# Scores of four query tiles in one run of six PSUM banks: a hybrid attention block on one Trainium2 core

## The chip, the cores and the metric

The kernel runs on one core of one Trainium2 chip. A core has five engines with queues of their own that work side by side: TensorE (PE) multiplies matrices, VectorE (DVE), ScalarE (ACT) and GpSimd (POOL) work element by element, SyncE (SP) issues the transfers (DMA). Matmul results land in PSUM, which the program uses as eight banks of 128 partitions by 512 single-precision columns; everything else lies in SBUF. The metric is the device time of one execution in microseconds (us); the median of three runs of the kernel before is 594.63 (594.57 to 594.85).

## The reference

One layer of a decoder block over 512 positions of width 1024, with 16 learned "meta" positions set in front (528 keys). Two attentions of 16 heads each run on the same normed input: MLA (queries and keys from low-rank latents, with a rotary part) and a "forgetting" attention (FoX below: a cumulative forget gate is added to the logits). Cut to what matters:

```python
u = rmsnorm(h, pre_norm_g[l])
proj = u @ w_in[l]                      # cq, ckv, k_pe, z_mla, fq, fk, fv, f_logit, z_fox, gates
q = (rmsnorm(cq) @ w_uq[l])...          # 16 heads: 64 + 32 rotary
kv = (rmsnorm(ckv) @ w_ukv[l])...       # 16 heads: 64 keys, 64 values
o_mla = causal_block_attention(q_m, k_m, v_mla, MLA_SCALE)
y_mla = (o_mla * silu(z_mla)) @ w_br_mla[l]
cum = cumsum(log_sigmoid(f_logit + fox_forget_b))
o_fox = causal_block_attention(fq, fk, fv, FOX_SCALE, cum)   # logit[t,s] += cum[t] - cum[s]
y_fox = (o_fox * silu(z_fox)) @ w_br_fox[l]
mixed = (sigmoid(gate_a) * y_mla + sigmoid(gate_b) * y_fox) @ w_out[l]
h = h + rmsnorm(mixed, post_norm_g[l])
```

The attention takes 128 queries at a time: query tile b (0 to 3) sees 144 + 128 b keys, 144, 272, 400 and 528.

## The kernel before

**Precision.** Every projection is done in three passes of fast-precision operands: weights and inputs are split into a high and a low part (`wh`, `wl`, `uTh`, `uTl`), and high x high, high x low, low x high are summed. ACT makes the high half of each 128 x 1024 block of weights (L130), POOL, or DVE where `low[0]` says so, the low half (L103). The same split makes `hlq`, `hlk` out of queries and keys.

**Stages.** The attention part runs over 16 stages, `stages = [(br, pr) for pr in range(NH // 2) for br in (1, 0)]`: pair of heads pr, FoX (br 1) and then MLA (br 0). Only PE's order is written out by hand; the other engines' queues are ordered by a scheduler from the order of the code, from priorities (`high_priority`) and from pins (`issue_after`), SP's transfers in program order. In a stage PE does:

- `scores(0)`: both heads side by side, one on each half of the array's rows (64 of 128), for query tiles 0, 1 and 2. Three pairs of matmuls for each piece in FoX, five in MLA (two for the rotary part, `QP`). Tiles 0 and 1 share a bank for each head (144 + 272 columns), tile 2 has one for each head (400 columns);
- `late`: the values' products `ov` of the stage before, 26 matmuls that use the array as two column halves, into the one bank of `ovp`;
- `scores(1)`: tile 3, 528 columns as 272 + 256 in two banks for each head;
- the fill: projections for the stage to come (q, k, v: `fq`, `fk`, `mq`, `mk`, `v`) and z, in steps of three matmuls. Their accumulators come from `accp`, three banks in rotation (`acc`).

PSUM so holds 3 banks `acc`, 4 banks `stp` in rotation for the scores and 1 bank `ovp`.

**Behind the scores.** DVE adds mask or forget bias, scales, and takes the row minimum in one pass out of PSUM (L784: `sf`, `nb`; the masks are `maskt`, or `cbp` and its masked copy `cbm`); ACT takes exponentials with their sums (L792); DVE the reciprocals (L800, L801). `norm(0)` (tiles 0 to 2) and `norm(1)` (tile 3) write the normed weights as a high and a low half-precision part: ACT L819 the high, DVE L820 the low, POOL the columns of the meta positions (the "lead", L806 to L811). Four DMA transposes for each stage (`pt<-pn`) bring them to the layout that the values' products need. `masked_bias` (POOL, L860 and L861) makes `cbm` for the next FoX stage behind the lead of `norm(1)`.

**Readers of the accumulators.** `hl_done` splits q and k out of the `acc` bank (ACT L244 high, DVE L103 low). v's two banks are read by DVE for the maximum (L688), by ACT (L701, L707) and by DVE (L710). z goes through ACT and DVE (L723, L724).

**Stage 0.** Before the loop stand the first k, q and v and a unit of gate projections (`gate_unit`, 8 steps of three matmuls, `pg`): four steps before the loop, three between `scores(0)` and `scores(1)`, one behind. Stage 0 has no values before it; their first products run in stage 1.

Of the kernel before, what the change touches and what calls it, by code (L numbers as in the profile page):

```python
# [25 lines left out]
L = S + META  # L26
# [19 lines left out]
HALF = 272  # L46
ROW = 64
# [7 lines left out]
def block_kernel(ctx: ExitStack, tc: tile.TileContext, x, meta_tokens, pre_norm_g, w_in, fox_forget_b,  # L55
# [119 lines left out]
    def unit(name, getw, act, nk, sls, done):  # L175
# [8 lines left out]
        for i, sl in enumerate(sls):  # L184
            n = sl.stop - sl.start
            for k in range(nk):
                def fn(i=i, sl=sl, k=k, n=n):
# [4 lines left out]
                    if k == 0:  # L192
                        st["ps"] = acc(f"{name}{i}")
# [11 lines left out]

    REAL = [slice(META, L)]
# [44 lines left out]
    def k_fox(pr):  # L251
        return unit(f"fk{pr}", win_w(O_FK, pr), u_act, KD, ALLT, hl_done(("k", 1, pr), L, HALF))

# [286 lines left out]
    with ExitStack() as att:  # L540
# [4 lines left out]
        stp = att.enter_context(tc.tile_pool(name="stp", bufs=4, space=PSUM))  # L545
        ovp = att.enter_context(tc.tile_pool(name="ovp", bufs=1, space=PSUM))

# [120 lines left out]
        def k_mla(pr):  # L668
            return unit(f"mk{pr}", lambda: by_k(mw[pr][2], 1), ckv_act, 1, ALLT, hl_done(("k", 0, pr), L, HALF))

        vsc = {}

        def v_unit(br, pr):
# [41 lines left out]
            return unit(f"v{br}{pr}", get, act, nk, ALLT, done), [(0, tr)]  # L715
# [15 lines left out]
        def attention(br, pr):  # L731
# [30 lines left out]
            def scores(g):  # L762

                banks = (((0, 0, 144, 0), (1, 0, 272, 144)), ((2, 0, 400, 0),)) if g == 0 else \
                    (((3, 0, HALF, 0),), ((3, HALF, L - HALF, 0),))

                def fn():
                    if g == 0:
                        for t in ("nb", "su", "ri"):
                            sums[t] = aw.tile([128, 2, 4], F32, tag=t, name=f"{t}{nm_}")  # L770
                    sfs[g] = aw.tile([128, 2, (2 * SF_STEP + 400, L)[g]], F32, tag=f"sf{g}", name=f"sf{nm_}{g}", bufs=1)
                    for ib, parts in enumerate(banks):
                        ps = [stp.tile([128, 512], F32, tag="st", name=f"st{nm_}{g}{ib}{h}") for h in range(2)]
                        for b, c0, w, o in parts:
                            for i, ops in enumerate(zip(*(sets(h, b, c0, w) for h in range(2)))):
                                for h, (Q, K) in enumerate(ops):
                                    mm(ps[h][:, o : o + w], Q, K, start=(i == 0), stop=(i == last_set))
                        for b, c0, w, o in parts:
                            for h in range(2):
                                nb = sums["nb"][:, h, b : b + 1]  # L780
                                for a, e, in1 in added(h, b, c0, c0 + w):

                                    with tc.high_priority(offset=100):
                                        nc.vector.tensor_tensor_reduce(  # L784
                                            out=sf_of(h, b)[:, a:e], in0=ps[h][:, o + a - c0 : o + e - c0],
                                            in1=in1, scale=-scale, scalar=3.0e38 if a == 0 else nb,
                                            op0=ALU.add, op1=ALU.min, accum_out=nb)
                    with tc.high_priority(offset=60):
                        for b in GRP[g]:
                            for h in range(2):  # L790
                                sf = sf_of(h, b)
                                exps[g] = nc.scalar.activation(sf, sf, AF.Exp, bias=sums["nb"][:, h, b : b + 1],  # L792
                                                               scale=-1.0, accum_out=sums["su"][:, h, b : b + 1]).ins
                return fn
# [521 lines left out]
```

## Time and profile before

| | |
|---|---|
| median of the runs | 594.63 us (594.57 to 594.85) |
| the profiled execution | 594.53 us, span 592.4 us |
| busy: PE / DVE / ACT / POOL | 583.9 / 412.8 / 357.9 / 200.6 us |
| scores on PE (`st`), share of the chain | 8% |
| values on PE (`ov`), share of the chain | 5% |
| `mk` on PE, share of the chain | 1% |

A row of the timeline is: start and length in us, engine, line, operation, written tile <- read tiles, shape, count. For PE "64*128" is a matmul on half the array's rows and "80*64" or "128*64" one on half its columns; the length of a matmul is modelled and overlaps the next, so the distance between two starts is the better measure. In square brackets stands how long the engine was idle before, and what ended it. A row of the chain is: start, length, engine, tile, line, number of instructions.

### The profile page before, as it was taken

What the parts mean: (1) busy time and instruction counts of PE and PEld (TensorE: products, weight loads), DVE (VectorE), ACT (ScalarE), POOL (GpSimd) and SP (SyncE); (2) the same over time, 40 slices, a digit from 0 to 9 for tenths busy, and PEclk for the clock granted to TensorE, in tenths of its full rate; (3) what the DMA queues carried; (4) which work ended last, traced back from release to release, by engine and by line L of the source; (5) the groups of instructions that cost most, each with busy time, mean ns of one, the idle gap of its engine ahead of it and who ended that gap; (6) DMA issues with size and microseconds to landing.
All of it is one profiled execution on the core that took longest, in us unless ns stands there. A gap on an engine that the chain in (4) does not pass through costs nothing.

```text
span 592.4 us, 11129 instructions
## 1 busy us (share of the span) xinstructions
PE 583.9 (99%) x3841; PEld 500.1 (84%) x3841; DVE 412.8 (70%) x1155; ACT 357.9 (60%) x816; POOL 200.6 (34%) x271
## 2 busy tenths in 40 slices
PE   8999999999999999999999999999999999999996
PEld 6889789889889888888898897888998998888884
DVE  5854876775775776666758748797647777468957
ACT  6946775784774784766748748764444363443753
POOL 4317746455458463554544544420000000000000
PEclk9999999999999999999999999999999999999999
DMA  8535599999994998997995986866822534333603
GB/s 282 125 88 164 120 176 251 225 184 237 168 205 111 229 205 197 213 182 179 185 202 147 203 160 147 193 138 215 273 72 71 143 97 134 91 106 106 214 2 142
DMA packets 220000, 97.47 MB, mean 165 GB/s; under 512 B 131456, under 2 KB 209672, under 8 KB 219944
## 3 DMA queue, kind: packets, MB, share of 16 engines
q1 hardware_dynamic: 219944, 96.77, 69.1%
q8 instruction: 30, 0.49, 0.3%
q14 instruction: 26, 0.21, 0.1%
HBM read 62.36 MB, written 3.97 MB: 112 GB/s over the span
## 4 chain that ended last, share of the span: by engine, by line
PE 97%; DMA 1%; DVE 1%; ACT 0%; SPq 0%; issue 0%; POOL 0%; DVEq 0%; POOLq 0%
PE z L97 19%; PE pg L97 15%; PE v L97 9%; PE st L97 8%; PE fk L97 8%; PE fq L97 8%; PE x L97 8%; PE py L97 7%; PE ov L97 5%; PE psm L97 3%; PE y L97 2%; PE mq L97 2%; PE mk L97 1%; PE ppe L97 1%; DMA wsr<-in_w_in_dram 1%; PE pt L100 0%
## 5 line engine op out<-in xcount | busy, mean ns | idle before, releaser
L103 POOL TENSOR_TENSOR wl<-wraw,wh 128x1024 fp32r<-128x1024 f32 (+2 forms) x62 | 120.3, 1948 | 96.3 <-ACT wh L130 74.0
L130 ACT CAST wh<-wraw 128x1024 fp32r<-128x1024 f32 (+1 forms) x72 | 74.6, 1040 | 53.5 <-PE py L97 16.8
L792 ACT ACTIVATE sf<-sf,nb 128x272 f32<-128x272 f32 (+3 forms) x128 | 72.5, 568 | 17.1 <-DVE nb L784 15.6
L820 DVE SCALAR_TENSOR_TENSOR pn<-sf,ri,pn 128x128 f16<-128x128 f32 (+3 forms) x128 | 68.6, 576 | 7.3 <-ACT pn L819 7.1
L103 DVE TENSOR_TENSOR wl<-wraw,wh 128x512 fp32r<-128x512 f32 (+1 forms) x54 | 51.0, 947 | 27.5 <-ACT wh L1053 18.9
L819 ACT ACTIVATE pn<-sf,ri 128x128 f16<-128x128 f32 (+3 forms) x128 | 61.2, 549 | 9.9 <-ACT sf L792 7.9
L97 PE MATMUL z<-uTh,wh 128*128 128x512 f32 x128 | 51.0, 398 | 0.0
L97 PE MATMUL pg<-uTh,wh 128*128 128x512 f32 x128 | 50.3, 393 | 0.0
L97 PE MATMUL z<-uTl,wh 128*128 128x512 f32 x128 | 50.1, 392 | 0.0
L97 PE MATMUL z<-uTh,wl 128*128 128x512 f32 x128 | 50.0, 391 | 0.0
L97 PE MATMUL pg<-uTl,wh 128*128 128x512 f32 x128 | 49.9, 390 | 0.0
L97 PE MATMUL pg<-uTh,wl 128*128 128x512 f32 x128 | 49.9, 389 | 0.0
L97 PE MATMUL st<-hlk,hlq 64*128 64x272 f32 (+3 forms) x480 | 45.5, 308 | 0.0
L1053 ACT CAST wh<-wraw 128x512 fp32r<-128x512 f32 x28 | 17.3, 619 | 39.8 <-DVE wraw L1062 15.4
L688 DVE TENSOR_REDUCE vsc<-v 128x1 f32<-128x272 f32 (+1 forms) x32 | 13.2, 433 | 39.9 <-PE v L97 39.9
L97 PEld LDWEIGHTS st<-hlk,hlq 64*128 64x128 f32 x480 | 34.5, 185 | 6.0 <-ACT vh L707 2.8
L97 PE MATMUL v<-uTh,wl 128*128 128x256 f32 (+1 forms) x128 | 36.5, 285 | 0.0
L97 PE MATMUL fk<-uTl,wh 128*128 128x256 f32 (+1 forms) x128 | 36.5, 285 | 0.0
L97 PE MATMUL fk<-uTh,wh 128*128 128x256 f32 (+1 forms) x128 | 36.4, 285 | 0.0
L97 PE MATMUL v<-uTl,wh 128*128 128x256 f32 (+1 forms) x128 | 36.4, 285 | 0.0
L97 PE MATMUL fk<-uTh,wl 128*128 128x256 f32 (+1 forms) x128 | 36.4, 285 | 0.0
L97 PE MATMUL v<-uTh,wh 128*128 128x256 f32 (+1 forms) x128 | 36.4, 284 | 0.0
(285 smaller groups left out, 1612.7 us busy)
## 6 DMA issues: line engine op xcount, KB each, us to landing
wraw<-in_w_in_dram SPq DMA_DIRECT2D x56, 512.0 KB, 4.7
cbp<-c_dram SPq DMA_DIRECT2D x16, 264.0 KB, 4.3
wraw<-in_w_br_fox_dram SPq DMA_DIRECT2D x8, 512.0 KB, 4.2
tb<-in_w_out_dram SPq DMA_DIRECT2D x8, 512.0 KB, 5.2
wraw<-in_w_br_mla_dram SPq DMA_DIRECT2D x8, 512.0 KB, 3.9
wraw<-in_w_out_dram SPq DMA_DIRECT2D x6, 512.0 KB, 3.8
xr<-in_x_dram SPq DMA_DIRECT2D x4, 512.0 KB
out_dram<-yo SPq DMA_DIRECT2D x8, 256.0 KB, 2.0
```

Of the source, the lines that this page charges most:

```text
L97: nc.tensor.matmul(*a, **k)
L103: return eng.tensor_tensor(out=lo, in0=src, in1=f32(hi), op=ALU.subtract)
L130: nc.scalar.copy(wh[:, :n], raw[:, :n])
L688: nc.vector.tensor_reduce(out=sc[:, i : i + 1], in_=ps, op=ALU.max, axis=AX.X, apply_absolute_value=True)
L792: exps[g] = nc.scalar.activation(sf, sf, AF.Exp, bias=sums["nb"][:, h, b : b + 1], scale=-1.0, accum_out=sums["su"][:, h, b : b + 1]).ins
L819: normed[:] = [nc.scalar.activation(hi, sf, AF.Copy, scale=rib).ins]
L820: nc.vector.scalar_tensor_tensor(out=lo, in0=sf, scalar=rib, in1=hi, op0=ALU.mult, op1=ALU.subtract)
L1053: nc.scalar.copy(to[0], src)
```

## The change

`stp` gets four banks with names of their own, b0, b1, c0, c1, instead of four in rotation. The scores of a stage become one run into six banks, three for each head: two `acc` banks hold tile 1 (272) and the first 240 columns of tile 3, b0 and b1 tile 0 (144) and tile 3's other 288, c0 and c1 tile 2 (400). The values' products of the stage before come behind that run and the fill behind them. Outside the scores the named banks serve as accumulators: FoX keys' first half in b0 (the second in `acc`), MLA keys' halves in b0 and b1, v's halves in c0 and c1. The exponentials are written in the order of tiles 1, 0, 2, 3. In stage 0 all eight gate steps stand ahead of the scores. The line numbers move by 1 to 10.

```diff
--- before.py
+++ after.py
@@ -44,6 +44,7 @@
 SF_STEP = 272
 PN_STEP = 5
 HALF = 272
+CUT = 240
 ROW = 64
 
 
@@ -172,7 +173,7 @@
 
     ths = {}
 
-    def unit(name, getw, act, nk, sls, done):
+    def unit(name, getw, act, nk, sls, done, banks=None):
 
         st = {}
         out = []
@@ -190,7 +191,7 @@
                         for load in getattr(out[0][1], "nxt", ()):
                             load()
                     if k == 0:
-                        st["ps"] = acc(f"{name}{i}")
+                        st["ps"] = (banks or acc)(f"{name}{i}")
                     ps = st["ps"][:, :n]
                     (wh, wl), (ah, al) = st["w"], act(k)
                     for q, (w, a) in enumerate(((wh, ah), (wh, al), (wl, ah))):
@@ -203,6 +204,7 @@
             out[0][1].load = getw.load
         return out
 
+    keybank = [None]
     REAL = [slice(META, L)]
     ALLT = [slice(0, HALF), slice(HALF, L)]
 
@@ -249,7 +251,7 @@
         return unit(f"fq{pr}", win_w(O_FQ, pr), u_act, KD, REAL, hl_done(("q", 1, pr), S, S))
 
     def k_fox(pr):
-        return unit(f"fk{pr}", win_w(O_FK, pr), u_act, KD, ALLT, hl_done(("k", 1, pr), L, HALF))
+        return unit(f"fk{pr}", win_w(O_FK, pr), u_act, KD, ALLT, hl_done(("k", 1, pr), L, HALF), keybank[0])
 
 
 
@@ -542,8 +544,16 @@
         att.enter_context(tc.manual_schedule(engines={mybir.EngineType.PE}))
         ac = att.enter_context(tc.tile_pool(name="ac", bufs=1))
         aw = att.enter_context(tc.tile_pool(name="aw", bufs=2))
-        stp = att.enter_context(tc.tile_pool(name="stp", bufs=4, space=PSUM))
+        stp = att.enter_context(tc.tile_pool(name="stp", bufs=1, space=PSUM))
         ovp = att.enter_context(tc.tile_pool(name="ovp", bufs=1, space=PSUM))
+
+        def bank(tag):
+            return lambda name: stp.tile([128, 512], F32, tag=tag, name=name)
+
+        def two(tag):
+            return lambda name: bank(tag + name[-1])(name)
+
+        keybank[0] = lambda name: bank("b0")(name) if name[-1] == "0" else acc(name)
 
         cb = [[thp.tile([128, L], F32, tag="th", name=f"cb{n}{h}") for h in range(2)] for n in "pm"]
         QP = ac.tile([128, S], F32R, tag="QP", name="QP")
@@ -666,7 +676,7 @@
         mw = {}
 
         def k_mla(pr):
-            return unit(f"mk{pr}", lambda: by_k(mw[pr][2], 1), ckv_act, 1, ALLT, hl_done(("k", 0, pr), L, HALF))
+            return unit(f"mk{pr}", lambda: by_k(mw[pr][2], 1), ckv_act, 1, ALLT, hl_done(("k", 0, pr), L, HALF), two("b"))
 
         vsc = {}
 
@@ -712,7 +722,7 @@
 
             def tr():
                 dma(vps[br], vh.rearrange("p t c -> p (t c)"), nc.sync.dma_start_transpose)
-            return unit(f"v{br}{pr}", get, act, nk, ALLT, done), [(0, tr)]
+            return unit(f"v{br}{pr}", get, act, nk, ALLT, done, two("c")), [(0, tr)]
 
         sils = {}
 
@@ -759,39 +769,36 @@
                 d = META + 128 * b if b else 0
                 return [(a, e, cb[n][h][:, a:e]) for n, a, e in ((0, c0, min(c1, d)), (1, max(c0, d), c1)) if a < e]
 
-            def scores(g):
-
-                banks = (((0, 0, 144, 0), (1, 0, 272, 144)), ((2, 0, 400, 0),)) if g == 0 else \
-                    (((3, 0, HALF, 0),), ((3, HALF, L - HALF, 0),))
-
-                def fn():
-                    if g == 0:
-                        for t in ("nb", "su", "ri"):
-                            sums[t] = aw.tile([128, 2, 4], F32, tag=t, name=f"{t}{nm_}")
+            def scores():
+
+                for t in ("nb", "su", "ri"):
+                    sums[t] = aw.tile([128, 2, 4], F32, tag=t, name=f"{t}{nm_}")
+                for g in range(2):
                     sfs[g] = aw.tile([128, 2, (2 * SF_STEP + 400, L)[g]], F32, tag=f"sf{g}", name=f"sf{nm_}{g}", bufs=1)
-                    for ib, parts in enumerate(banks):
-                        ps = [stp.tile([128, 512], F32, tag="st", name=f"st{nm_}{g}{ib}{h}") for h in range(2)]
-                        for b, c0, w, o in parts:
-                            for i, ops in enumerate(zip(*(sets(h, b, c0, w) for h in range(2)))):
-                                for h, (Q, K) in enumerate(ops):
-                                    mm(ps[h][:, o : o + w], Q, K, start=(i == 0), stop=(i == last_set))
-                        for b, c0, w, o in parts:
-                            for h in range(2):
-                                nb = sums["nb"][:, h, b : b + 1]
-                                for a, e, in1 in added(h, b, c0, c0 + w):
-
-                                    with tc.high_priority(offset=100):
-                                        nc.vector.tensor_tensor_reduce(
-                                            out=sf_of(h, b)[:, a:e], in0=ps[h][:, o + a - c0 : o + e - c0],
-                                            in1=in1, scale=-scale, scalar=3.0e38 if a == 0 else nb,
-                                            op0=ALU.add, op1=ALU.min, accum_out=nb)
-                    with tc.high_priority(offset=60):
-                        for b in GRP[g]:
-                            for h in range(2):
-                                sf = sf_of(h, b)
-                                exps[g] = nc.scalar.activation(sf, sf, AF.Exp, bias=sums["nb"][:, h, b : b + 1],
-                                                               scale=-1.0, accum_out=sums["su"][:, h, b : b + 1]).ins
-                return fn
+                for rooms, parts in (([acc, acc], ((1, 0, 272, 0), (3, 0, CUT, 272))),
+                                     ([bank("b0"), bank("b1")], ((0, 0, 144, 0), (3, CUT, L - CUT, 144))),
+                                     ([bank("c0"), bank("c1")], ((2, 0, 400, 0),))):
+                    ps = [room(f"st{nm_}{parts[0][0]}{h}") for h, room in enumerate(rooms)]
+                    for b, c0, w, o in parts:
+                        for i, ops in enumerate(zip(*(sets(h, b, c0, w) for h in range(2)))):
+                            for h, (Q, K) in enumerate(ops):
+                                mm(ps[h][:, o : o + w], Q, K, start=(i == 0), stop=(i == last_set))
+                    for b, c0, w, o in parts:
+                        for h in range(2):
+                            nb = sums["nb"][:, h, b : b + 1]
+                            for a, e, in1 in added(h, b, c0, c0 + w):
+
+                                with tc.high_priority(offset=100):
+                                    nc.vector.tensor_tensor_reduce(
+                                        out=sf_of(h, b)[:, a:e], in0=ps[h][:, o + a - c0 : o + e - c0],
+                                        in1=in1, scale=-scale, scalar=3.0e38 if a == 0 else nb,
+                                        op0=ALU.add, op1=ALU.min, accum_out=nb)
+                with tc.high_priority(offset=60):
+                    for b in (1, 0, 2, 3):
+                        for h in range(2):
+                            sf = sf_of(h, b)
+                            exps[b // 3] = nc.scalar.activation(sf, sf, AF.Exp, bias=sums["nb"][:, h, b : b + 1],
+                                                                scale=-1.0, accum_out=sums["su"][:, h, b : b + 1]).ins
 
             def norm(g):
                 def fn():
@@ -838,7 +845,7 @@
                 nc.vector.scalar_tensor_tensor(out=gT[br][:, pr, :], in0=po, scalar=vsc[br, pr], in1=sils[br, pr],
                                                op0=ALU.mult, op1=ALU.mult)
 
-            return scores(0), scores(1), norm(0), norm(1), values
+            return scores, norm(0), norm(1), values
 
         def stores(a, b):
 
@@ -887,8 +894,7 @@
         pe0, rest0, store0 = pe_unit(0)
         pe_rest = [(0, lambda x=x: rest0(x)) for x in range(2)]
         g = gate_unit()
-        first = pe0 + v + [(0, in_order)] + g[:4]
-        begun = g[4:]
+        first = pe0 + v + [(0, in_order)] + g
         fills = []
         for si, (br, pr) in enumerate(stages):
             last = si + 1 == len(stages)
@@ -897,7 +903,7 @@
             if br == 1:
 
                 za, zb = z_unit(1, pr), z_unit(0, pr)
-                fill = (vts[br, pr] if pr else begun) + za + q + zb[:3] + k + zb[3:5] + v + zb[5:]
+                fill = (vts[br, pr] if pr else []) + za + q + zb[:3] + k + zb[3:5] + v + zb[5:]
             elif not last:
 
                 fill = vts[br, pr] + q + k[:KD] + v + k[KD:]
@@ -921,34 +927,31 @@
         lctx.close()
         gpool = gctx.enter_context(tc.tile_pool(name="gpool", bufs=1, side="right"))
         gT += [gpool.tile([128, KD, S], F32, tag=n, name=n) for n in ("gT0", "gT1")]
-        run(first[len(pe0) : -4])
+        run(first[len(pe0) : -KD])
         behind[:] = [halved[("k", 1, 0), 1]]
-        run(first[-4:])
+        run(first[-KD:])
         behind.clear()
         late = []
         for si, (br, pr) in enumerate(stages):
             last = si + 1 == len(stages)
-            s0, s1, n0, n1, va = attention(br, pr)
+            sc, n0, n1, va = attention(br, pr)
 
             fill = fills[si]
-            for fn in [s0] + late:
+            sc()
+            for fn in late:
                 fn()
             if si == 0:
-                run(fill[:3])
-            s1()
-
-            if si == 0:
-
-                run(fill[3:5])
+
+                run(fill[:1])
                 run(vts[1, 0] + pe_rest)
                 n0()
                 bias(1)
                 low[0] = nc.vector
-                for ahead_ in [fn.prep for _, fn in fill[5:] if hasattr(fn, "prep")][:2]:
+                for ahead_ in [fn.prep for _, fn in fill[1:] if hasattr(fn, "prep")][:2]:
                     ahead_()
                 low[0] = nc.gpsimd
                 n1()
-                run(fill[5:])
+                run(fill[1:])
             else:
                 if si == 1:
                     stores(2, 4)
```

PE at the start of stage 1 (MLA). `st` are score banks, one number for each head, `ov` the values' bank; `z` is the projection ahead, `fq` the one behind. Before, from tile 2's last matmul through the values to tile 3 (the rows between repeat):

```order
L97 MATMUL st_1153<-KPL,QP 128x400
L97 MATMUL st_1154<-KPL,QP 128x400
...
L97 MATMUL ov_1173<-pt,vp_720 64x128
L97 MATMUL st_1202<-hlk_1074,hlq_1055 128x272
L97 MATMUL st_1203<-hlk_1074,hlq_1055 128x272
...
L97 MATMUL st_1202<-KPL,QP 128x272
L97 MATMUL st_1203<-KPL,QP 128x272
L97 MATMUL st_1216<-hlk_1074,hlq_1055 128x256
L97 MATMUL st_1217<-hlk_1074,hlq_1055 128x256
```

Now:

```order
L98 MATMUL z_1058<-uTh,wl_1005 128x512
L98 MATMUL st_1126<-hlk_1072,hlq_1053 128x272
L98 MATMUL st_1127<-hlk_1072,hlq_1053 128x272
...
L98 MATMUL st_1178<-KPL,QP 128x400
L98 MATMUL st_1179<-KPL,QP 128x400
L98 LDWEIGHTS vp_720
L98 MATMUL ov_1200<-pt,vp_720 64x512
...
L98 MATMUL ov_1200<-pt,vp_720 64x128
L98 MATMUL fq_1239<-uTh,wh_1233 128x512
```

The 272 and 256 columns of tile 3 stood between the values and the projection; now the values follow tile 2's 400 columns and the projection follows the values.

DVE in stage 0, behind the reads of v (`vh`) and ahead of the first reads of scores (ISA, `sf`). Before:

```order
L710 SCALAR_TENSOR_TENSOR vh<-v_814,vsc_812,vh 128x2x128
L784 ISA sf_873,nb_870<-st_874,cbm_707 128x144
L784 ISA nb_870 128x1
...
L784 ISA sf_921,nb_870<-st_933,cbm_708,nb_870 128x128
L784 ISA nb_870 128x1
L800 TENSOR_SCALAR su_871<-su_871 128x2x3
L801 RECIPROCAL ri_872<-su_871 128x2x3
L103 TENSOR_TENSOR wl_1007<-wraw_855,wh_1006 128x1024
```

Now:

```order
L720 SCALAR_TENSOR_TENSOR vh<-v_814,vsc_812,vh 128x2x128
L104 TENSOR_TENSOR wl_1005<-wraw_855,wh_1004 128x1024
L792 ISA sf_887,nb_884<-st_889,cbp_705 128x144
L792 ISA nb_884 128x1
L792 ISA sf_887,nb_884<-st_889,cbm_707,nb_884 128x128
L792 ISA nb_884 128x1
L792 ISA sf_888,nb_884<-st_889,cbp_705 128x240
```

The split of the weights `wl` that read `wraw_855` stood behind all reads of scores and the sums; now it is ahead of the first read.

POOL in stage 1: `mt` and `pn` are the lead columns (96 wide for tiles 0 to 2, 32 for tile 3), `wl` splits of the weights that `fk` (`wraw_1046`, now 1044) and `v` (`wraw_1058`, now 1056) of the same stage's fill use, `cbm` the masked bias. Before:

```order
L806 TENSOR_TENSOR mt_1258<-sf_1126,ri_1125 128x96
L809 CAST pn_715<-mt_1258 128x2x3x16
L811 CAST pn_715<-mt_1258 128x2x3x16
L810 TENSOR_TENSOR pn_715<-mt_1258,pn_715 128x2x3x16
L103 TENSOR_TENSOR wl_1294<-wraw_1046,wh_1293 128x1024
L103 TENSOR_TENSOR wl_1349<-wraw_1058,wh_1348 128x1024
L806 TENSOR_TENSOR mt_1312<-sf_1201,ri_1125 128x32
L809 CAST pn_716<-mt_1312 128x2x16
L811 CAST pn_716<-mt_1312 128x2x16
L810 TENSOR_TENSOR pn_716<-mt_1312,pn_716 128x2x16
L860 COPY cbm_707<-cbp_705 128x16
L861 AFFINE_SELECT cbm_707<-cbp_705 128x512
```

Now:

```order
L813 TENSOR_TENSOR mt_1308<-sf_1125,ri_1123 128x32
...
L817 TENSOR_TENSOR pn_716<-mt_1308,pn_716 128x2x16
L867 COPY cbm_707<-cbp_705 128x16
L868 AFFINE_SELECT cbm_707<-cbp_705 128x512
L867 COPY cbm_708<-cbp_706 128x16
L868 AFFINE_SELECT cbm_708<-cbp_706 128x512
L104 TENSOR_TENSOR wl_1290<-wraw_1044,wh_1289 128x1024
L813 TENSOR_TENSOR mt_1254<-sf_1124,ri_1123 128x96
...
L817 TENSOR_TENSOR pn_715<-mt_1254,pn_715 128x2x3x16
L104 TENSOR_TENSOR wl_1345<-wraw_1056,wh_1344 128x1024
```

Tile 3's lead and the masked bias went ahead of both splits, and the lead of tiles 0 to 2 between them.

## The prediction

> **What bounds the kernel now.** First the page's busy line and the chain that ended last.
>
> ```profile
> PE 583.9 (99%) x3841; PEld 500.1 (84%) x3841; DVE 412.8 (70%) x1155; ACT 357.9 (60%) x816; POOL 200.6 (34%) x271
> PE 97%; DMA 1%; DVE 1%; ACT 0%; SPq 0%; issue 0%; POOL 0%; DVEq 0%; POOLq 0%
> ```
>
> TensorE (PE) is the chain. A change can gain only by shortening PE's own sequence or by removing the few waits inside it, and it loses wherever PE comes to wait. So I read PE's starts one by one. This is the chain of waits at the start of a FoX stage (start, length, in us):
>
> ```profile
> 143.94 1.45 PE st L97 x18
> 145.38 1.97 PE ov L97 x26
> 147.35 1.11 PE st L97 x12
> ```
>
> Scores of tiles 0 to 2, the values' products of the stage before, scores of tile 3: 1.45 + 1.97 + 1.11 = 4.53. The timeline of PE shows the same start of an MLA stage operation by operation (start, length as modelled; the lengths overlap, so I use differences of starts):
>
> ```profile
> 120.29 0.39 PE L97 MATMUL z<-uTl,wh 128*128 128x512 f32 x1
> 120.52 0.39 PE L97 MATMUL z<-uTh,wl 128*128 128x512 f32 x1
> 120.84 0.56 PE L97 MATMUL st<-hlk,hlq 64*128 64x144 f32 x6
> 121.45 0.58 PE L97 MATMUL st<-hlk,hlq 64*128 64x272 f32 x6
> 122.12 0.71 PE L97 MATMUL st<-hlk,hlq 64*128 64x400 f32 x6
> 123.13 2.04 PE L97 MATMUL ov<-pt,vp 80*64 80x512 f16 x26
> 125.10 0.65 PE L97 MATMUL st<-hlk,hlq 64*128 64x272 f32 x6
> 126.18 0.28 PE L97 MATMUL st<-KPH,QP 64*128 64x256 f32 x2
> 126.30 0.28 PE L97 MATMUL st<-KPL,QP 64*128 64x256 f32 x2
> 126.51 0.50 PE L97 MATMUL fq<-uTh,wh 128*128 128x512 f32 x1
> 126.84 0.40 PE L97 MATMUL fq<-uTl,wh 128*128 128x512 f32 x1
> ```
>
> Projections run on the whole array and 0.23 us apart; scores use it as two row halves (64*128), values as two column halves (80*64). Each change of shape shows: 0.32 instead of 0.23 before the scores, 0.33 between the first two fq. From first st to first fq the stage takes 126.51 − 120.84 = 5.67.
>
> **The change part by part.**
>
> *One run of scores in an MLA stage, eight times.* The second run, 125.10 to 126.51, takes 1.41. Without a change of shape around it the same 272 columns took 0.67 (121.45 to 122.12) and the 256 columns cost 5 pairs at 0.12 (126.18 to 126.30) = 0.60, so 0.14 of it is entry and exit. The entry into the first run and its exit into the values stay, and so do the first slow fq intervals, provided that values followed by a projection cost what they do here, late in the program:
>
> ```profile
> 399.61 2.04 PE L97 MATMUL ov<-pt,vp 80*64 80x512 f16 x26
> 401.58 0.50 PE L97 MATMUL pg<-uTh,wh 128*128 128x512 f32 x1
> ```
>
> They do: 1.97 to the next start, as ahead of the scores (123.13 to 125.10). Tile 3 as 240 + 288 columns instead of 272 + 256 is the same sum, and a 272 instead of a 144 at the head I estimate at 0.01 dearer. I take 0.13 a stage: 8 x 0.13 = 1.0. Bounds: 0 (the exit comes back behind the values) and 0.2 each (entry and exit both go whole).
>
> *The same in a FoX stage, seven times* (stage 0 apart), with a wait on top. The same twelve matmuls that take 1.11 at 147.35 stand in stage 0, where no values come before them, at
>
> ```profile
> 63.30 0.99 PE L97 MATMUL st<-hlk,hlq 64*128 64x272 f32 x12
> 64.22 0.50 PE L97 MATMUL pg<-uTh,wh 128*128 128x512 f32 x1
> 147.44 0.34 DVE L784 CUSTOM_DVE_ANT_0 sf<-st,cbm,nb 128x128 f32<-128x128 f32 x1
> ```
>
> 0.92: the other 0.19 is a wait for a bank. Tile 3's second half takes the banks of tile 2, and VectorE (DVE) lets go of them only after the last read, 147.44 to 147.78. In six separate banks that wait has no object. 0.19 + 0.14 = 0.33 a stage: 7 x 0.33 = 2.3. Bounds 0.19 and 0.4 each.
>
> *Stage 0's two runs become one.* There both runs lie between projections, so one whole set of entry and exit goes: 0.09 ahead of the scores and 0.10 behind the first projection, as in the MLA rows, and within the run 0.92 less 3 x 0.12 + 3 x 0.13 = 0.75, that is 0.17. I take 0.34, with bounds 0.17 and 0.36.
>
> *Keys' accumulators leave the common banks.* The chain has eight pieces of six mk matmuls; the first two and the last:
>
> ```profile
> 74.11 0.74 PE mk L97 x6
> 115.74 0.98 PE mk L97 x6
> 369.59 0.94 PE mk L97 x6
> ```
>
> In stage 0 they take 0.74; the other seven 0.98, 0.98, 0.89, 0.94, 0.92, 0.96, 0.94: 1.43 of waiting, for the bank that mq's low half is still read from. Now each half has a score bank, drained long before. −1.4, bounds −1.4 and 0 (if hlq's readers hold something else).
>
> Sum of PE's gains: 1.0 + 2.3 + 0.34 + 1.4 = 5.1; by the bounds 1.5 to 6.2.
>
> *What may come late: accumulators of v in tile 2's banks.* DVE's last reads of v in an MLA stage:
>
> ```profile
> 120.85 1.02 DVE L710 SCALAR_TENSOR_TENSOR vh<-v,vsc,vh 128x16 f16<-128x16 f32 x3 [0.72 <-ACT vh L707]
> ```
>
> v is read by 121.87. Tile 2 will start some 2.6 behind 120.84 (0.67 + 0.6 + 0.6 + 0.7), at 123.4: slack 1.6, so the cost is nothing, and if v is read later, what exceeds 1.6. In a FoX stage tile 2 comes 2.0 after the start and v has been read sooner before it, slack about 1.5.
>
> *What will come late: stage 0.* All four late gate steps now stand ahead of the scores: 4 x 3 x 0.23 = 2.8, so the scores start at 62.3 instead of 59.56. And the split of the next weights (wl, 1.23) now stands in DVE's queue ahead of the scores' reads.
>
> ```profile
> 65.03 1.05 ACT L130 CAST wh<-wraw 128x1024 fp32r<-128x1024 f32 x1 [0.44 <-issue]
> 65.80 0.69 DVE L800 TENSOR_SCALAR su<-su 128x6 f32<-128x6 f32 x1
> 66.62 1.23 DVE L103 TENSOR_TENSOR wl<-wraw,wh 128x1024 fp32r<-128x1024 f32 x1
> 56.61 0.38 SPq L91 DMA_DIRECT2D wraw<-in_w_in_dram  x1
> wraw<-in_w_in_dram SPq DMA_DIRECT2D x56, 512.0 KB, 4.7
> 69.24 9.27 SPq L91 DMA_TRANSPOSE pt<-pn  x4
> 81.26 2.04 PE L97 MATMUL ov<-pt,vp 80*64 80x512 f16 x26
> 144.99 0.31 DVE L784 CUSTOM_DVE_ANT_0 sf<-st,cbm 128x144 f32<-128x144 f32 x1 [0.18 <-PE st L97]
> 149.90 0.35 DVE L784 CUSTOM_DVE_ANT_0 sf<-st,cbm,nb 128x128 f32<-128x128 f32 x1
> ```
>
> Those weights are asked for at 56.61 and land, by the median 4.7, near 61.3 to 62.3; ScalarE's (ACT) half 1.05, then DVE's 1.23: 64.5. DVE's reads of one FoX stage take 150.25 − 144.99 = 5.3 with a gap for the values between, some 4.5 without it: 69.0 (68.0 if the split is early, 69.8 with the 5.3). Before, they had ended when the sums began, 65.80, and the first transpose came 3.44 later, at 69.24. The same distance gives 72.4, and tile 2's exponentials, now the last, may add some tenths: I take 72.7, a shift of 3.5. The four hold SP's queue 9.27, before until 78.51, and the values stood at 81.26: the margin is 2.75 less the unshown landing of the last one, so between 0 and 2.75. Values now come behind all scores, 3.6 instead of 2.3 behind the stage's start, which itself is 0.34 sooner: 82.2, 1.0 later than before. Stall: 3.5 − 1.0 − (0 to 2.75) = 0 to 2.5; I take the middle, 1.1.
>
> *Behind it, in stage 1*, SP's next two weight loads are issued 3.5 later too, and POOL does tile 3's lead and the two masked biases ahead of the first weight split, and tiles 0 to 2's lead ahead of the second.
>
> ```profile
> 84.69 0.35 POOL L806 TENSOR_TENSOR mt<-sf,ri 128x96 f32<-128x96 f32 x1 [1.51 <-DVE ri L801]
> 85.93 5.01 POOL L103 TENSOR_TENSOR wl<-wraw,wh 128x1024 fp32r<-128x1024 f32 x2
> 93.53 0.69 POOL L860 COPY cbm<-cbp 128x16 f32<-128x16 f32 x1
> 95.42 0.64 POOL L861 TENSOR_SCALAR_AFFINE_SELECT cbm<-cbp 128x512 f32<-128x512 f32 x1
> 93.44 0.29 PE L97 MATMUL v<-uTh,wl 128*128 128x272 f32 x1
> ```
>
> Masks 93.53 to 96.06 = 2.5, tiles 0 to 2's lead 84.69 to 85.93 = 1.2, tile 3's by estimate two thirds of it, 0.8, splits 5.0: 9.5. This chain can begin when tile 3's sums are there; before, tile 0 to 2's were at 84.69, and I estimate 0.8 later for tile 3 in the longer run, 85.5, so the second split ends near 95.0 instead of 90.94. v's third matmul wants it at 93.44, moved by the gain of 0.5 and the stall of 1.1 to 94.1. Stall 0 to 1.8 (POOL's lengths are rough); I take 0.5.
>
> Sum: 594.53 (the profiled execution) − 5.1 + 1.6 = 591.0; it lies 0.1 under the median of the runs shown, 594.63, which I leave out.
>
> [...] The row-half rows show 0.09 to 0.15 at a change of shape. [...]
>
> **The rivals.**
>
> *The full gain, nothing late*: the margin behind the transposes is near 2.75 and POOL's splits come in time. 594.53 − 5.1 + 0.2 = 589.6. For it: the margin is not bounded from below by a row. Against it: a shift of 3.5.
>
> *The start ripples*: stall 2.5 at the values, 1.8 at v: 594.53 − 5.1 + 4.3 = 593.7. For it: both come from one late queue, and each was bounded by rows. Against it: the second shrinks as the first grows.
>
> *DVE's emptying sets every stage (slower)*. PE writes six banks in 2.6 (FoX) to 3.5 us (MLA), DVE reads a FoX stage's in 4.5, and tile 2, last read, must pass exponentials, reciprocals and norms before the first transposes. If these start later in every stage than the next values can bear, PE waits 15 times. The row is
>
> ```profile
> 152.85 8.46 SPq L91 DMA_TRANSPOSE pt<-pn  x4
> ```
>
> It decides once the transposes' queue, free at 161.31 there, stays busy up to the values; 0.23 us at each of 15 boundaries cancels what is left of the gain (3.5), and 0.6 at each is +9: 600. Against it: in that stage DVE's reads all end ahead of the norms already (150.25, first transpose 152.85), so tile 2 being last moves little, and values themselves come 1.0 to 1.3 later. [...]
>
> *Values into projections cost more than in the one place seen*: the exit returns 15 times at 0.14 to 0.2, −5.1 + 1.6 + 2.5 = 593.5.
>
> **How the numbers follow.** Forecast 0.55 (own range 590.0 to 592.2, mostly the two stalls), full gain 0.15, ripple 0.14, exits 0.07, slower 0.09. A measurement here tells 0.2%, 1.2 us, from no change: faster means under 593.4. Faster: 0.55 + 0.15 + half of the ripple and of the exits = 0.81; same: the other halves less a little, 0.09; slower 0.10. The range leaves out the slowest case and the far ends: 588.9 to 593.3.
>
> **What would show it.** In the profile of the changed kernel: 5.5 us (MLA) and 4.2 (FoX) from the first st to the first projection; six mk in 0.74 everywhere; no bank wait in st; PE idle ahead of ov near 82.2 by about 1, and ahead of v's third matmul near 94 by about 0.5; first transposes near 72.7. It is wrong if st waits for DVE in every stage, if the first projection after ov starts later than 1.97 behind it, or if the late transposes are still late in stage 2.

## The result, and the profile after

The changed kernel took 590.18 us (median of six, 589.89 to 592.53), the kernel before beside it 594.43 us (593.52 to 594.85): a ratio of 0.9939, 95% interval 0.9927 to 0.9952. Forecast were 591.0 us, with 588.9 to 593.3 as the range. In a later run beside other versions the same kernel took 591.32 us (590.74 to 592.51), ratio 0.9949 (0.9937 to 0.9961); its spread is taken up with the experiments on the clock.

The page's busy line and the chain that ended last, of the changed kernel:

```profile
span 587.9 us, 11120 instructions
PE 577.0 (98%) x3841; PEld 497.4 (85%) x3841; DVE 416.7 (71%) x1155; ACT 357.2 (61%) x816; POOL 200.4 (34%) x271
PE 90%; POOL 3%; DMA 2%; DVE 2%; ACT 1%; issue 1%; SPq 0%; DVEq 0%; POOLq 0%
```

TensorE is busy for 6.9 us less, but the span is shorter by only 4.5, and the chain now leaves PE in places. The chain of waits at an MLA stage, a FoX stage and at mk (start, length, in us) shows what was gained:

```profile
121.39 3.52 PE st L98 x50
124.91 1.97 PE ov L98 x26
126.88 0.43 PE fq L98
144.22 2.19 PE st L98 x30
146.41 1.97 PE ov L98 x26
148.37 1.81 PE z L98 x7
157.51 0.74 PE mk L98 x6
```

From the first score to the first projection an MLA stage takes 126.88 − 121.39 = 5.49 us instead of 5.67, a FoX stage 148.37 − 144.22 = 4.15 instead of 4.53, and mk 0.74 instead of 0.98. In stage 0, one run between two projections:

```profile
61.37 0.39 PE L98 MATMUL pg<-uTh,wl 128*128 128x512 f32 x1
61.69 2.26 PE L98 MATMUL st<-hlk,hlq 64*128 64x272 f32 x30
63.88 0.50 PE L98 MATMUL z<-uTh,wh 128*128 128x512 f32 x1
```

2.19 us, where the two runs took 1.46 and 0.92; the second entry and exit beside the projections, 0.2, went too.

And this is where some of it went back: the timelines of SyncE, VectorE and TensorE at the start, and the chain there.

```profile
72.59 8.35 SPq L92 DMA_TRANSPOSE pt<-pn  x4
62.69 1.36 DVE L104 TENSOR_TENSOR wl<-wraw,wh 128x1024 fp32r<-128x1024 f32 x1 [3.32 <-ACT wh L131]
77.59 6.00 DMA pt<-pn
83.73 2.04 PE L98 MATMUL ov<-pt,vp 80*64 80x512 f16 x26 [2.21 <-DMA pt<-pn]
```

The first transpose starts at 72.59 instead of 69.24, the last lands at 77.59 + 6.00 = 83.59, and TensorE stands idle for 2.21 us (2.3 between starts) before the first values.

The sum: 8 x 0.18 + 7 x 0.38 + 0.39 + 1.43 = 5.9 gained, 2.3 lost to the wait and 0.08 ahead of v: 3.5 net. The ratio makes 3.6 of 594.4; the medians lie 4.2 apart, the two profiled executions 4.5. Of these 4.5 us some 0.6 lies ahead of all changed work: the last gate matmul starts at 61.37, where 59.24 plus the four steps moved ahead (2.76) would make 62.0. The 0.4 that is left is spread over the stages, a few hundredths in each, and is not assigned to a cause.

### The profile page after: what moved, and what is told of

The parts are those of the page before. It is cut to its first block, busy times and chain, and to the rows that moved or that the text cites. A ratio compares the mean times of both kernels' runs of the same rounds, so it can differ in the third digit from the quotient of the medians.

```text
span 587.9 us, 11120 instructions
## 1 busy us (share of the span) xinstructions
PE 577.0 (98%) x3841; PEld 497.4 (85%) x3841; DVE 416.7 (71%) x1155; ACT 357.2 (61%) x816; POOL 200.4 (34%) x271
## 4 chain that ended last, share of the span: by engine, by line
PE 90%; POOL 3%; DMA 2%; DVE 2%; ACT 1%; issue 1%; SPq 0%; DVEq 0%; POOLq 0%
PE z L98 17%; PE pg L98 14%; PE v L98 8%; PE x L98 8%; PE fq L98 8%; PE fk L98 8%; PE py L98 7%; PE st L98 7%; PE ov L98 5%; PE psm L98 3%; PE y L98 2%; PE mq L98 2%; POOL wl L104 1%; DMA pt<-pn 1%; PE mk L98 1%
## 5 line engine op out<-in xcount | busy, mean ns | idle before, releaser
L800 ACT ACTIVATE sf<-sf,nb 128x272 f32<-128x272 f32 (+3 forms) x128 | 72.7, 569 | 10.9 <-DVE nb L792 10.1
L827 DVE SCALAR_TENSOR_TENSOR pn<-sf,ri,pn 128x512 f16<-128x512 f32 (+3 forms) x128 | 71.5, 625 | 2.4 <-ACT pn L826 2.4
L826 ACT ACTIVATE pn<-sf,ri 128x512 f16<-128x512 f32 (+3 forms) x128 | 59.6, 548 | 0.0
L98 PE MATMUL st<-hlk,hlq 64*128 64x272 f32 (+4 forms) x480 | 41.3, 299 | 0.0
L98 PEld LDWEIGHTS st<-hlk,hlq 64*128 64x128 f32 x480 | 33.0, 186 | 4.1 <-ACT vh L717 2.1
```

The costliest lines, as they stand in the source:

```text
L98: nc.tensor.matmul(*a, **k)
L800: exps[b // 3] = nc.scalar.activation(sf, sf, AF.Exp, bias=sums["nb"][:, h, b : b + 1], scale=-1.0, accum_out=sums["su"][:, h, b : b + 1]).ins
L826: normed[:] = [nc.scalar.activation(hi, sf, AF.Copy, scale=rib).ins]
L827: nc.vector.scalar_tensor_tensor(out=lo, in0=sf, scalar=rib, in1=hi, op0=ALU.mult, op1=ALU.subtract)
```

## The experiments

All of them start from the changed kernel.

**Gate steps back where they were.**

```diff
-        first = pe0 + v + [(0, in_order)] + g
+        first = pe0 + v + [(0, in_order)] + g[:4]
+        begun = g[4:]          # run behind the scores of stage 0
```

> The changed kernel, with stage 0's gate steps as before: four ahead of the scores, four behind them. My theory: the 2.2 us that TensorE waits ahead of the first values' products (81.5 to 83.7 in the changed kernel) comes from the scores of stage 0 starting 2.8 us later and from the split of weights ahead of their reads; with both gone the first transposes start near 69 instead of 72.6, TensorE does not wait there, and the time falls by 2.0 us (0.3 may come back at z, whose weights are now split later): 588.2. Rival: the transposes are late for another reason (their own landing, traffic): the wait stays above 1 us and the time within 0.7 us of the changed kernel's 590.2.

Measured 589.55 us (589.40 to 591.78), ratio 0.9927 (0.9914 to 0.9941). The wait ahead of the first values is gone, as expected, but only 0.6 us came back where 2.0 were expected; the time alone would have fitted the rival. The queue and what TensorE waited for instead:

```profile
68.79 9.60 SPq L92 DMA_TRANSPOSE pt<-pn  x4
71.85 0.50 PE L98 MATMUL z<-uTh,wl 128*128 128x512 f32 x1 [0.19 <-DVE wl L104]
94.00 0.39 PE L98 MATMUL v<-uTh,wl 128*128 128x272 f32 x1 [1.02 <-POOL wl L104]
```

0.3 to 0.4 between starts went to z, as foreseen, and 1.2 to v's third matmul, which was not. GpSimd's timeline shows why:

```profile
85.84 0.64 POOL L868 TENSOR_SCALAR_AFFINE_SELECT cbm<-cbp 128x512 f32<-128x512 f32 x1
87.17 2.39 POOL L104 TENSOR_TENSOR wl<-wraw,wh 128x1024 fp32r<-128x1024 f32 x1
89.53 0.79 POOL L813 TENSOR_TENSOR mt<-sf,ri 128x96 f32<-128x96 f32 x1
91.39 2.56 POOL L104 TENSOR_TENSOR wl<-wraw,wh 128x1024 fp32r<-128x1024 f32 x1
```

Masks, first split, lead, second split: the order that the prediction named, ending at 93.95. In the changed kernel the second split ends at about the same time, and v's third matmul costs only 0.08 more than its neighbours (0.21 instead of 0.13 to the next start). From the timelines of GpSimd and TensorE in the changed kernel:

```profile
91.81 2.58 POOL L104 TENSOR_TENSOR wl<-wraw,wh 128x1024 fp32r<-128x1024 f32 x1
94.46 0.38 PE L98 MATMUL v<-uTh,wl 128*128 128x272 f32 x1
```

There TensorE comes late anyway, because it has waited for the values. One late chain covered the other.

**The early split of weights off VectorE.** The line `low[0] = nc.vector` ahead of the early splits is left out, so GpSimd does that one.

> The changed kernel, with the one early split of weights on GpSimd instead of VectorE, so that VectorE reads stage 0's scores from about 62.9 on instead of 64.0; all eight gate steps stay ahead. My theory: the transposes start 1.1 us sooner and the wait ahead of the first values shrinks from 2.2 to 1.1: 589.1. Rival (only the gates count, the reads have slack): no change, 590.2. Rival (GpSimd's lead columns come late behind the split): slower by up to 1 us.

Measured 590.23 us (590.17 to 590.86), ratio 0.9933 (0.9921 to 0.9945).

```profile
63.05 0.31 DVE L792 CUSTOM_DVE_ANT_0 sf<-st,cbp 128x144 f32<-128x144 f32 x1 [3.32 <-PE st L98]
72.14 8.54 SPq L92 DMA_TRANSPOSE pt<-pn  x4
83.46 2.04 PE L98 MATMUL ov<-pt,vp 80*64 80x512 f16 x26 [1.60 <-DMA pt<-pn]
71.58 0.54 POOL L817 TENSOR_TENSOR pn<-mt,pn 128x96 f16<-128x96 f32 x1
```

and in the changed kernel:

```profile
72.16 0.40 POOL L817 TENSOR_TENSOR pn<-mt,pn 128x96 f16<-128x96 f32 x1
```

VectorE starts 1.0 after the scores instead of 2.3, but the transposes come only 0.8 sooner and the wait shrinks by 0.6, to 1.60. Exponentials and norms do follow VectorE: ScalarE begins the norms at 69.31 instead of 70.23, 1.3 sooner counted from the scores. The first transpose, though, starts 0.02 to 0.03 behind the end of GpSimd's lead of tiles 0 to 2 in both kernels (72.12 and 72.56). That lead starts only 0.9 sooner, since tile 3's lead stands ahead of it until 70.2, and takes 1.9 instead of 1.7. So GpSimd's lead is what comes late, as in the third rival, but not because of the split, which had ended at 68.6, and without making the kernel slower. The forecast of 1.1 was too much. The time itself is that of the first rival (590.2): 0.6 is not told from the changed kernel there, since the beginnings of executions differ by about as much (0.6 between the profiled ones of the kernel before and the changed kernel), and it is the trace that speaks against this rival.

**Two runs again, in the six banks.** Values go between tile 3's second part and tile 2.

```diff
+                    if parts[0][0] == 2:
+                        for fn in mid:          # the values of the stage before
+                            fn()
                     ps = [room(f"st{nm_}{parts[0][0]}{h}") for h, room in enumerate(rooms)]
```

> The changed kernel with its six banks, but with the values' products put between tile 3's second part and tile 2: two runs of scores again in every stage. My theory: each of 15 stages pays one entry and one exit, 0.19 us as the traces of before and after differ without the bank wait, 2.8 us; and the first values are wanted 1.1 us sooner while the transposes land as late, so 1.1 more: 594.1. In FoX stages the score matmuls show no bank wait. Rival (what was gained in a stage is the bank wait and the order, not the changes of shape): at most 1.1 us slower, 591.3.

Measured 599.71 us (597.83 to 601.64), ratio 1.0094 (1.0077 to 1.0111): slower than the kernel before. The stages without a wait show what was asked for, an MLA and a FoX stage from the timeline of TensorE:

```profile
127.24 0.65 PE L98 MATMUL st<-hlk,hlq 64*128 64x272 f32 x6
132.92 0.50 PE L98 MATMUL fq<-uTh,wh 128*128 128x512 f32 x1
150.26 1.71 PE L98 MATMUL st<-hlk,hlq 64*128 64x272 f32 x24
154.60 0.50 PE L98 MATMUL z<-uTh,wh 128*128 128x512 f32 x1
```

MLA 5.68: as much as the kernel before (5.67), 0.19 more than the changed kernel. FoX 4.34: 0.19 more than the changed kernel, 0.19 less than the kernel before. So an entry and an exit cost 0.19 in either kind of stage, the bank wait in FoX stages cost 0.19, and the six banks and other widths by themselves change nothing in an MLA stage. This part of the theory holds to the hundredth. The time does not: it is 5.6 us above the 594.1 expected. Where it went:

```profile
85.28 3.45 PE L98 MATMUL ov<-pt,vp 80*64 80x512 f16 x26 [3.22 <-DMA pt<-pn]
85.20:88.50 3.30, 3.22 (x25) 2.01 (x26) 0.00 (x0) 1.06 (x4) 0.00 (x0) 0.55 0.90 271
171.88 0.62 PE L98 MATMUL ov<-pt,vp 80*64 80x512 f16 x4 [0.53 <-DMA pt<-pn]
```

The first values wait 3.22, and behind that wait the same 26 matmuls take 3.4 instead of 2.0 us: in the second row, which is a stretch of the table by windows (length, busy time of PE, PEld, DVE, ACT, POOL, then the granted clock of TensorE, DMA share and GB/s), the clock is 0.55. And three later MLA stages wait ahead of their values as well (0.53 for a transpose here, then 0.62 and 0.81, for which the trace names nothing), and in stage 1 fk waits 1.36 for a split of GpSimd. Late transposes are what the prediction's third rival feared, but in a kernel that wants its values 1.0 us sooner than the changed one and has tile 2's scores behind them; which of the two makes them late is not separated.

**MLA keys' accumulators back in the common banks.** `two("b")` is left out of `k_mla`.

> The changed kernel with MLA keys' accumulators back in the three common banks. By the trace of the changed kernel the low half of mq is read until 76.16 in stage 0 and 118.61 in stage 2, 2.9 and 1.9 us behind the start of mk's second half, and 0.05 behind it in six later stages. My theory: stage 0 waits 2.9, which takes the place of the 2.2 us wait ahead of the first values, stage 2 waits 2.0, six stages 0.1 each: +3.3 us, 593.5. Rival (the wait is what it was in the kernel before): +1.4 us, 591.6. Rival (the bank is not what mk waited for): no change.

Measured 597.1 us (596.41 to 597.43), ratio 1.0045 (1.0033 to 1.0057): 7 us above the changed kernel, twice what was expected.

```profile
76.23 0.40 PE L98 MATMUL mk<-cTh,wh 128*128 128x272 f32 x1 [2.47 <-DVE sil L734]
78.06 0.63 PE L98 MATMUL z<-uTl,wh 128*128 128x512 f32 x1
76.20:80.00 3.80, 3.77 (x12) 3.22 (x13) 1.44 (x3) 0.76 (x2) 0.00 (x0) 0.55 1.12 209
98.38 0.39 PE L98 MATMUL v<-uTh,wl 128*128 128x272 f32 x1 [1.00 <-POOL wl L104]
121.65 0.39 PE L98 MATMUL mk<-cTh,wh 128*128 128x272 f32 x1 [1.25 <-DVE sil L734]
163.19 0.93 PE mk L98 x6
162.76 0.68 DVE L104 TENSOR_TENSOR hlq<-mq,hlq 128x512 fp32r<-128x512 f32 x1
163.50 0.38 PE L98 MATMUL mk<-cTh,wh 128*128 128x256 f32 x1
```

It is a bank that mk waits for, in every stage. In stages 0 and 2 it is that of z, read by VectorE behind the norms (2.47 and 1.25), where the expectation had mq's. In the six later stages it is mq's, as expected, with 0.2 each instead of 0.1: in the last two rows the second half of mk starts at 163.50, behind VectorE's read of mq, which ends at 163.44. The wait of stage 0 takes the place of the one ahead of the first values, as expected. What the expectation lacked: z's matmuls right behind it take 0.43 each (78.06 to the next at 78.49) instead of 0.23, at a clock of 0.55 over 3.8 us, and v's wait of 1.0 at 98.38 shows as soon as nothing hides it.

**The transposes made later by one more.** In stage 0 tile 0's transpose is issued twice.

> The changed kernel, with stage 0's first transpose (tile 0) issued twice: the three others start 1.35 us later, nothing else moves. My theory: the wait ahead of the first values is the landing of the last transpose, so it grows from 2.2 to 3.6 us; and since TensorE showed a granted clock near half for some 3.5 us behind waits of 2.6 and 3.3 us in two other runs, but not behind 2.2, such a stretch follows here and costs another 1.7: 593.2. Rival (the wait is priced at its own length): 591.5. Rival (the transposes are not what the values wait for): 590.2.

Measured 594.59 us (593.87 to 595.32), ratio 1.0006 (0.9997 to 1.0015).

```profile
72.85 11.39 SPq L92 DMA_TRANSPOSE pt<-pn  x5
80.85 5.11 DMA pt<-pn
86.10 3.63 PE L98 MATMUL ov<-pt,vp 80*64 80x512 f16 x26 [4.41 <-DMA pt<-pn]
85.00:89.00 4.00, 2.90 (x18) 1.74 (x20) 0.54 (x3) 1.85 (x6) 2.26 (x8) 0.62 0.92 248
```

The wait grew by 2.2, to 4.41, more than the 1.35 of the extra transpose: from the first issue to the last of the five lie 8.00 (72.85 to 80.85), 3.0 more than between those of the four in the changed kernel (72.59 to 77.59; why is not shown), and the last one landed 5.11 after its issue instead of 6.00. Behind it the values take 3.6 instead of 2.0, at a clock of 0.62 over 4 us. Together 3.8, and 4.4 in the time. Both parts of the theory hold, the size of the first was too small. The executions differ in their mean clock too: 0.994 to 0.996 at 593.9 to 594.3, 0.991 to 0.992 at 594.6 to 595.3. The profiled one is of the first kind, so what the others have beside its one slow stretch is not known.

**The changed kernel again**, beside the next one.

> The changed kernel itself, on the same chip and in turn with the next two, so that the three can be compared. Its wait ahead of the first values lay at 2.2 us in its profile, close under the 2.5 behind which the clock fell elsewhere; my theory: most executions near 590.0, some of them about 1.7 us longer with a lower mean clock (0.995 instead of 0.998). Rival: no such second group.

Measured 591.32 us (590.74 to 592.51). Its profiled execution took 591.32 with a mean clock of 0.994. The same place in this execution, and the stretch behind the wait in the first one:

```profile
83.56 3.13 PE L98 MATMUL ov<-pt,vp 80*64 80x512 f16 x26 [2.06 <-DMA pt<-pn]
87.22 0.63 PE L98 MATMUL fq<-uTl,wh 128*128 128x512 f32 x1
84.00:88.00 4.00, 4.00 (x28) 3.10 (x25) 2.17 (x8) 3.94 (x11) 2.61 (x9) 0.57 0.79 238
```

```profile
84.00:88.00 4.00, 4.00 (x36) 3.24 (x33) 2.07 (x8) 4.00 (x11) 2.63 (x9) 1.00 1.18 228
```

The wait is even shorter, 2.06 against 2.21, but here the clock falls to 0.57 in the mean of these 4 us, where it was 1.00, and 28 matmuls run instead of 36: about 1.4 us more by the time that stage 2 begins (v in stage 1 starts at 95.67 instead of 94.21). So a wait of 2.1 to 2.2 us cost its length in one execution of this kernel and 1.4 us on top in another. The two groups that the theory expected show only in part. Over both sets of executions, the three at a mean clock of 0.994 or 0.995 took 591.3, 591.7 and 592.5, as slow as expected or slower; but the eight at 0.997 to 0.999 took anything from 589.9 to 592.5, half of them over 590.7, and in this set none came near 590.0. So the clock is not the whole of the spread, and the rest is open.

**Four gate steps ahead, again**, in turn with the changed kernel.

> The kernel with four gate steps ahead and four behind, again. From the traces it is 0.7 us shorter than the changed kernel between the first scores and stage 3; with no long wait left its executions should not show the lower clock: 589.4. Rival: no difference to the changed kernel within 0.2 us.

Measured 589.76 us (589.37 to 590.21), ratio 0.9921 (0.9909 to 0.9933), clocks 0.998 and 0.999: the interval lies below that of the changed kernel in the same turn, 0.9937 to 0.9961. This version beats both kernels. Of the 1.6 us between the two medians the traces explain 0.7 without the clock; that the long wait, behind which the clock fell to 0.57 in one of two profiled executions, makes up the rest is likely but not shown, since the changed kernel's executions without the lower clock lie above this version too.

**Stage 1 put in order by hand**, in the version with four gate steps ahead: ScalarE's halves of k's and v's weights ahead of the norms, on GpSimd the lead ahead of the second split (`issue_after(lead)`), the masked bias behind both splits.

> The kernel of the run with four gate steps ahead, with stage 1 put in order by hand: ScalarE's high halves of k's and v's weights ahead of the norms, GpSimd's lead columns of tiles 0 to 2 ahead of the second split, the masked bias behind both splits. My theory: the 1.2 us by which that kernel waits at v's third matmul (92.8 to 94.0) is GpSimd's queue, in which the masked biases (1.5 us) stand ahead of the splits and the second split waits for ScalarE; with that gone v does not wait and up to 0.6 may come back ahead of stage 2's values, whose transposes then land close to when they are wanted: 0.6 to 1.2 us faster than that kernel, 588.4 to 589.0. Rival: the wait moves whole to stage 2's values: no change, 589.5.

> The kernel with stage 1 put in order by hand, again. From the traces 1.3 us shorter than the changed kernel between the first scores and stage 3: 588.8, and no execution with the lower clock. Rival: the same time as the kernel with four gate steps behind the scores.

Measured 589.23 us (588.92 to 589.72, four executions), ratio 0.9917 (0.9903 to 0.993); the second time 590.17 us (588.85 to 593.29, six), 0.9937 (0.9918 to 0.9955). In the first one's profile v no longer waits, and what is left in stages 0 and 1 is

```profile
71.63 0.50 PE L98 MATMUL z<-uTh,wl 128*128 128x512 f32 x1 [0.17 <-DVE wl L104]
82.22 2.04 PE L98 MATMUL ov<-pt,vp 80*64 80x512 f16 x26 [0.31 <-DMA pt<-pn]
```

The trace has what was expected, 1.3 us less than the changed kernel from the first scores up to stage 3, and 0.6 less than with the gate steps alone. The times do not: the second one is 1.4 above the expected 588.8, and one execution did show a lower mean clock, 0.995 at 593.3; two more took 590.5 and 590.6 at 0.997 and 0.999, and none of these three was profiled. So it is not shown to be faster than the version with the gate steps alone, and why its times spread stays open.

## Why the prediction was right, point by point, and what it had wrong

- **TensorE's sequence bounds the kernel**: right; every gain of the sum was found in the starts of TensorE's matmuls, and every loss as a wait between them.
- **One run in an MLA stage, 0.13**: the mechanism was right, the term mis-sized. It measured 0.18, and the run with two runs in six banks gives 0.19 for one entry and exit. The prediction took the second run's cost without a change of shape as 0.67 + 0.60; that was about 0.05 too much, perhaps because it is put together from short rows rounded to 0.01 us.
- **One run in a FoX stage, 0.33, of it 0.19 a bank wait**: 0.38, by the same run 0.19 bank wait and 0.19 entry and exit. The wait was named and sized rightly; the other part has the error of the MLA term.
- **Stage 0, 0.34**: 0.39.
- **mk, 1.4**: 1.43, all eight at 0.74. The lower bound, "0 if hlq's readers hold something else", did not cover what would come: with the readers late behind six banks, leaving mk where it was cost 7 us in the run, the lower clock included. The term was right as a difference to the kernel before, but that bank is a condition of the change rather than an addition to it.
- **v in tile 2's banks**: no wait shows in any stage, as predicted.
- **Stage 0's transposes**: "I take 72.7" measured 72.59, by luck: the whole execution began 0.6 earlier, and counted from the first scores the transposes came 0.5 later than forecast (10.9 instead of 10.4).
- **The stall, 1.1**: 2.2. This is the largest error. What was wrong is the margin, of which the prediction took the middle of 0 and 2.75. The last transpose lands 6.0 us after its issue, 2.65 behind the end of its row in the queue; the same added to the kernel before, 75.16 + 6.0 = 81.2, leaves hardly 0.1 ahead of the values at 81.26 (an estimate, since no row shows that landing). The other terms were nearer but not exact: the last transpose was issued 2.4 later instead of 3.5, TensorE was ready for the values 0.2 later instead of 1.0, and 0.6 of either difference is the earlier beginning. 2.4 − 0.2 = 2.2 leaves no margin. The bound, 2.5, held.
- **v in stage 1, 0.5**: 0.08 in the changed kernel. GpSimd's chain ended at 94.39 instead of 95.0 (9.1 long instead of 9.5; the masked biases took 1.5 instead of 2.5, the lead of tiles 0 to 2 1.9 instead of 1.2), and the longer first wait brought TensorE there later. The chain itself was the one predicted; where the first wait is gone, TensorE stood idle for it 1.02, 1.00 and 0.67 us in three runs.
- **Luck in the number.** Gains of 5.1 + 0.8 more, stalls of 1.6 + 0.7 more: the errors were of one size and opposite sign, so that the measured terms put into the same sum give 591.0 again. That the time came out within 1 us owes something to this; the result lies below 591.0 by the earlier beginning and the 0.4 that is not assigned.
- **Not in the prediction**: the clock behind a wait, 0.57 over 4 us and about 1.4 us more in one of the two profiled executions of the changed kernel.
- **The rivals.** The full gain did not come; the ripple came in part, its first half; entries and exits did not return. VectorE's emptying does not set the stages of the changed kernel: from the first score to the first projection they take 4.15 and 5.49, 0.38 and 0.18 less than before. The run with the values 1.0 us sooner and tile 2 behind them shows that late transposes are near: there three MLA stages wait 0.5 to 0.8 ahead of their values, one of them, by the trace, for a transpose. "Values themselves come 1.0 to 1.3 later", which the prediction set against that rival, fits what keeps it away.

## What to carry to other kernels

Read a transfer's margin to its landing, not to the end of its row in the queue; where the profile has no row for the landing, take the margin as small, not as the middle. A median over all such transfers does not help either: for the 64 transposes of the kernel before it is 4.3 us, while the last one of stage 0 took 5.1 to 6.4 in the four traces that show it. When a change removes one wait from a full engine, look for the next chain that this wait covered, and price it as if uncovered. And a wait on TensorE can cost more than its length, here 1.4 us on top of one of 2.06 and nothing on top of one of 2.21: look at the granted clock behind it, and compare several executions.

## What the runs showed of the hardware

- Behind waits of 2.47, 3.22 and 4.41 us on TensorE the granted clock was 0.55, 0.55 and 0.62 in the mean of 3.8, 3.3 and 4.0 us behind (mk's accumulators in the common banks, two runs again, the transpose issued twice). In the first, matmuls of 512 columns came 0.43 instead of 0.23 apart; in the two others the values took 3.4 and 3.6 instead of 2.0. In the two profiled executions of the changed kernel the clock fell to 0.57 in the mean of 4 us behind a wait of 2.06 and was 1.00 behind one of 2.21. Behind one of 1.60 (the split on GpSimd) the first projection came 1.97 after the start of the values, as without a wait. Each fall cost about 1.4 to 1.7 us. From which wait on the clock falls, these executions do not show: one of 2.06 was enough once, one of 2.21 was not.
- One more run on row halves between column halves and the whole array costs TensorE 0.19 us, its entry and exit together (5.68 against 5.49 in an MLA stage, 4.34 against 4.15 in a FoX stage), the same with three and with five sets of operands. What TensorE does in that time the runs do not show.
- The last transpose of stage 0 landed 5.1 to 6.4 us after its issue in the four traces whose chain shows it: 6.00 in the changed kernel, 6.07 with the split on GpSimd, 5.11 with one transpose issued twice, 6.38 with stage 1 put in order by hand, the second time. In the first three it landed 2.65, 2.64 and 1.72 us behind the end of its row in the queue.
- In the changed kernel the four transposes of stage 0, into different places, are issued 1.35, 1.37 and 2.28 us apart, 5.00 from the first to the last. With the first issued twice into the same place, in one run, the five span 8.00.
